# Differential attention: four of nine probability blocks per query group multiplied with V in plain fp32

## The chip, the cores and the metric

One core of a Trainium2 chip runs the whole kernel. The metric is the device time of one execution in microseconds (us). Its engines are PE (TensorE: matmuls, with weight loads shown apart as PEld), DVE (VectorE), ACT (ScalarE), POOL (GpSimd) and SP (SyncE, which issues all DMAs here). Each engine takes its instructions in the order in which the program lists them.

## What is computed

One layer of a diffusion transformer with differential attention: 2048 latent tokens, 256 context tokens, width 1024, 8 heads. Each head has two score maps over 2304 keys; their softmaxes are subtracted with a weight and the result is multiplied with that head's values.

```python
q, k, v, z = split(rms_norm(x) * (1 + sc) + sh) @ w_in        # latent and context; rope on latent q, k
p = softmax(einsum('bqhzd,bkhzd->bhzqk', q * d**-0.5, k))
a = p[:, :, 0] - lam * p[:, :, 1]                             # 2048 x 2304 for each of 8 heads
o = einsum('bhqk,bkhe->bqhe', a, v)
o = o * rsqrt(mean(o*o) + eps) * subln_gain * (1 - lambda_init)
x = x + gt * ((o * silu(z)) @ w_out)                          # then a last rms_norm
```

## The kernel before, in words

All numbers are fp32. A product of two fp32 matrices is made on PE from three products of fp32r tiles, a format to which the producer of a tile rounds it: `hi` is the rounded value, `lo` is what is left (x - hi), and hi*hi + hi*lo + lo*hi is summed in PSUM.

Three stages follow one another. **project** (L178) normalizes the tokens, multiplies them with `w_in`, and writes q, k, v and the gate to scratch in DRAM. Values come from `mm_rows` (L423): 128 tokens x 256 columns (two heads) at a time, two such in a PSUM tile of 512 columns, that is 256 keys of two heads. There are 9 such tiles for each of 4 pairs of heads. `split_steps` (L481) cuts each into `hl` (high by ACT in `cut_high`, low by DVE in `cut_low`), and `store_rows` (L466) writes both halves to `v_d`, one DMA per head.

**attend** (L628) runs 64 query groups: 8 heads, and 8 groups of 256 queries in each. For a group there are 12 steps `qk` (four matmuls of 384 columns into one of two PSUM tiles `s`), each emptied by a `keep` on DVE (L683); exponentials on ACT (L701); a weight and a sum on POOL (L711, L715). The joined matrix, 256 queries x 2304 keys, is then taken in 9 blocks of 256 keys. For each block, `turn` transposes four 128x128 pieces on PE (L722) into a PSUM tile `t`; `high` copies it to an fp32r tile `hi` on ACT (L730); `low` makes t - hi on DVE (L735); and `pv` (L737) multiplies: for each of two key tiles three fp32r matmuls with 256 moving columns, the weights being V's high half (twice) and low half. Everything of a group accumulates in one PSUM tile `po`. `sumsq` (L773) is the one pair of matmuls that comes once in a group. After a head's eight groups, `mean` (L801 to L806) and `root` turn the sums of squares into a factor; these run among the next head's groups. During the last head, the gates of the first 512 tokens of heads 0 to 6 are worked in as well (`mul1` POOL L940, `mul2` DVE L944, `high` ACT L950, `low` DVE L954). **finish** (L957) is the output projection.

V of a head lies in SBUF, in one of two tiles `v`: high and low halves of 18 key tiles. `load_v` (L651) is called for heads 0 and 1 ahead of the loop, and for head h+2 after the last `pv` of head h. The same two tiles later hold output weights.

The order on each engine is set by `Plan.order` (L128): every step has a nominal length in ns, a due time, and buffers that it takes and gives back; a free engine starts the step that is due first among those whose inputs and buffers are there by the plan's own clock. For blocks these are

```python
step("low", "DVE", 602, due + 0.6, low, (g, b), [("high", g, b)], take=["LO"], give=["T"])
step("pv", "PE", 654, due + 2, pv, (g, b), [("low", g, b)] + first, give=["HI", "LO"])
```

with 3 buffers T (PSUM), 4 HI and 4 LO (SBUF).

Of the kernel before, what the change touches and what calls it, by code (L numbers as in the profile page):

```python
# [12 lines left out]
F32 = mybir.dt.float32  # L13
F32R = mybir.dt.float32r
# [6 lines left out]
P = 128  # L21
D = 1024
# [3 lines left out]
KEYS = LAT + CTX  # L26
KT = KEYS // P
# [13 lines left out]
S_BUFS = 2  # L41
T_BUFS = 3
A_BUFS = 6
TP_BUFS = 4
GD = 15
MIX, L3 = (1, 2), 15
XH, WH = 7, 7
# [3 lines left out]
def f32(ap):  # L51
    return ap.bitcast(F32)


def build(tc, x, c, ctx, c_ctx, norm_gain, ada_w, ada_b, final_gain, w_in,
          lam_q, lam_k, subln_gain, w_out, cos_t, sin_t, out):
    nc = tc.nc
    with ExitStack() as top:
        cp = top.enter_context(tc.tile_pool(name="const", bufs=1))
        dr = top.enter_context(tc.tile_pool(name="scratch", bufs=1, space=DRAM))  # L60

        q_d = [dr.tile([P, 2, LAT], F32, name=f"qd{h}") for h in range(H)]
        k_d = [dr.tile([P, 2, KEYS], F32, name=f"kd{h}") for h in range(H)]
        v_d = [dr.tile([P, 2, KT, P], F32, name=f"vd{h}") for h in range(H)]
# [12 lines left out]
        nc.vector.tensor_copy(ones, sums)  # L77
        mhalf = cp.tile([P, 16], F32, name="mhalf")
        nc.vector.memset(mhalf, -0.5)
        sgain = cp.tile([P, 1], F32, name="sgain")  # L80
        neglam = cp.tile([P, 1], F32, name="neglam")

        early = SimpleNamespace(qstack=top.enter_context(ExitStack()), kstack=top.enter_context(ExitStack()))

        def attend_early():
            early.qp = early.qstack.enter_context(tc.tile_pool(name="qp", bufs=1, side="right"))
            early.kp = early.kstack.enter_context(tc.tile_pool(name="kp0", bufs=1, side="right"))
            early.k = load_k(nc, early.kp, k_d, 0)
            early.q = load_q(nc, early.qp, q_d, 0)

        with ExitStack() as ph:
            project(tc, ph, attend_early, ones, x, ctx, c, c_ctx, norm_gain, ada_w, ada_b, w_in, lam_q, lam_k, subln_gain,
                    cos_t, sin_t, ident, mhalf, sgain, neglam, gt_d, q_d, k_d, v_d, gate_d, w_out, wo_d, sums)

        last = Last(tc, gate_d, o_d, f_d, wo_d)
        ph = top.enter_context(ExitStack())
        with ExitStack() as inner:
            attend(tc, ph, inner, early, last, ident, ones, mhalf, sums, neglam, q_d, k_d, v_d, o_d, s_d, f_d)
# [18 lines left out]

# [58 lines left out]


def project(tc, ph, attend_early, ones, x, ctx, c, c_ctx, norm_gain, ada_w, ada_b, w_in, lam_q, lam_k, subln_gain,  # L178
            cos_t, sin_t, ident, mhalf, sgain, neglam, gt_d, q_d, k_d, v_d, gate_d, w_out, wo_d, sums):
# [43 lines left out]

    tiles = {}

    # conditioning
    def cond_silu():
        nc.scalar.activation(rows[0:16], rows[0:16], AF.Silu)

# [79 lines left out]
        step("aturn", "PE", 120, due + 6, ada_turn, (n,), [("arow", n)], take=["AT"], give=["BR"], name=("aturn", n))  # L309
        step("acol", "DVE", 70, due + 6, ada_col, (n,), [("aturn", n)], give=["AT"])  # L310

    # rms norm, modulation and transposition of a block of tokens
    def x_load(b, t):
        src, row, nt = b.src
        xt = tiles["x", b.name, t] = xp.tile([P, D], F32, tag="x", name=f"x{b.name}_{t}", bufs=XB)
# [150 lines left out]
    def store_rows(nm, h, kt):  # L466
        hl = f32(tiles["hl", nm]).rearrange("p f (k u e) -> p f k u e", k=2, u=2)
        for u in range(2):
            nc.sync.dma_start(v_d[h + u][:, :, kt:kt + 2], hl[:, :, :, u])

    def z_silu(nm):
        gz = tiles["z", nm] = zp.tile([P, 512], F32, tag="z", name=f"z{nm}")
# [57 lines left out]
    for half, blks in enumerate(passes):  # L530
        for hpair in range(H // 2):
# [3 lines left out]
            for which, use in turns:  # L535
# [12 lines left out]
                for b in use:  # L548
# [7 lines left out]
                    for cc in range(nt // 2 if which == "v" else 2):  # L556
# [3 lines left out]
                        if which == "v":  # L560
                            for t in range(2):
                                step("mm", "PE", 2620, clock, mm_rows, (nm, w, b, 2 * cc, t), ready,
                                     take=["M"] if t == 0 else [], give=give if t == 1 else [], name=("mm", nm, t))
                                clock += 2.62
                            split_steps(nm, "m", 512, clock, [("mm", nm, 1)], ["M"], store_rows,
                                        (2 * hpair, b.key // P + 2 * cc))
# [58 lines left out]
    return qt  # L625


def attend(tc, ph, inner, early, last, ident, ones, mhalf, sums, neglam, q_d, k_d, v_d, o_d, s_d, f_d):  # L628
# [20 lines left out]
    unit = {}  # L649

    def load_v(h):  # L651
        head[h].v = vp.tile([P, 2, KT, P], F32R, tag="v", name=f"v{h}")
        for z in range(2):
            nc.sync.dma_start(f32(head[h].v[:, z]), v_d[h][:, z])

    def qk(g, u, z, ck):
        h, i = divmod(g, NG)
# [74 lines left out]
    def low(g, b):  # L732
        t = group[g].t[b]
        t[2] = tp.tile([P, 512], F32R, tag="lo", name=f"lo{g}_{b}")
        nc.vector.tensor_tensor(t[2], t[0], f32(t[1]), op=ALU.subtract)  # L735

    def pv(g, b):  # L737
        h = g // NG
        po = po2[:, g % 2]
        pt, hi, lo = group[g].t.pop(b)  # L740
        for e in range(KPER):
            kt = b * KPER + e
            for n, (vi, tt) in enumerate(((0, hi), (0, lo), (1, hi))):
                nc.tensor.matmul(po, head[h].v[:, vi, kt], tt[:, e * GQ:(e + 1) * GQ],  # L744
                                 start=(kt == 0 and n == 0), stop=(kt == KT - 1 and n == 2))
        if b == NB - 1 and g % NG == NG - 1 and h + 2 < H:
            load_v(h + 2)

# [69 lines left out]
        nc.vector.tensor_copy(ft, head[h].m[:n, :P])  # L818
        nc.sync.dma_start(f_d[h], ft)

    plan = Plan(S=S_BUFS, T=T_BUFS, A=A_BUFS, B=2, HI=TP_BUFS, LO=TP_BUFS, O=2)
    done = {}

    def step(kind, engine, cost, due, fn, args, deps=(), take=(), give=()):
# [3 lines left out]
    for g in range(TOTAL):  # L828
# [15 lines left out]
        for b in range(NB):  # L844
            due = (g + 1) * PER + LAG + b * PER / NB
            step("turn", "PE", 436, due, turn, (g, b), [("join", g, u) for u in range(G)],
                 take=["T"], give=["A"] * G if b == NB - 1 else [])
            step("high", "Activation", 478, due + 0.3, high, (g, b), [("turn", g, b)], take=["HI"])
            step("low", "DVE", 602, due + 0.6, low, (g, b), [("high", g, b)], take=["LO"], give=["T"])
            first = [("evac", g - 2)] if b == 0 and g > 1 else []  # L850
            step("pv", "PE", 654, due + 2, pv, (g, b), [("low", g, b)] + first, give=["HI", "LO"])
        due += 2
        step("evac", "Activation", 264, due + 2, evac, (g,), [("pv", g, NB - 1)])
        step("clamp", "Pool", 1029, due + 6, clamp, (g,), [("evac", g)])
# [33 lines left out]
    last.ps = ps_s  # L888
    last.f_turn, last.f_out = f_turn, f_out
    end = TOTAL * PER  # L890
    kshape, vshape = [P, 2, KEYS], [P, 2, KT, P]
# [11 lines left out]


class Last:
    """The gated and scaled heads that go into the output projection."""

    def __init__(self, tc, gate_d, o_d, f_d, wo_d):
        self.tc, self.nc = tc, tc.nc
# [10 lines left out]

    def weights(self, hs, pool, tag, shape):
        t = pool.tile(shape, F32R, tag=tag, name=f"wo{hs[0]}")
        flat = t.rearrange("p a b -> p (a b)" if len(shape) == 3 else "p a b c -> p (a b c)")
# [230 lines left out]
```

## Time and profile before

| | |
|---|---|
| time of three runs, us | 2357.25, 2364.41, 2365.6 (median 2364.41) |
| profiled execution: span | 2359.8 us (its own time is given as the span alone) |
| instructions | 38159 |
| PE busy / DVE busy / POOL busy / ACT busy | 95% / 73% / 60% / 52% of the span |
| granted TensorE clock, mean | 0.980 |
| project, attend, finish, by the trace | to about 829 us, to about 2169 us, to the end |

The page adds up busy time over three stages that have different limits, so the shares above are means over unlike things; the rows further below go by stage. PE's busy time is modelled from starts, so a PE that is shown as busy need not do as much as it can; the pace of its instructions, from start to start, is read from the chain of waits.

### The profile page before, as it was taken

What the parts mean: (1) busy time and instruction counts of PE and PEld (TensorE: products, weight loads), DVE (VectorE), ACT (ScalarE), POOL (GpSimd) and SP (SyncE); (2) the same over time, 40 slices, a digit from 0 to 9 for tenths busy, and PEclk for the clock granted to TensorE, in tenths of its full rate; (3) what the DMA queues carried; (4) which work ended last, traced back from release to release, by engine and by line L of the source; (5) the groups of instructions that cost most, each with busy time, mean ns of one, the idle gap of its engine ahead of it and who ended that gap; (6) DMA issues with size and microseconds to landing.
All of it is one profiled execution on the core that took longest, in us unless ns stands there. A gap on an engine that the chain in (4) does not pass through costs nothing.

```text
span 2359.8 us, 38159 instructions
## 1 busy us (share of the span) xinstructions
PE 2251.5 (95%) x14353; PEld 2070.0 (88%) x14353; DVE 1711.8 (73%) x3726; ACT 1220.0 (52%) x1717; POOL 1422.9 (60%) x691
## 2 busy tenths in 40 slices
PE   7999999999999989989989989899899899889998
PEld 5988888898888879989989989899899898788777
DVE  5746434453233289999999999999999999995664
ACT  5612312232112167767767767677677676564221
POOL 2523233343223268878878878878788788774643
PEclk9999999999999999999999999999999999899999
DMA  9965645454442251321311412213113114224672
GB/s 309 292 217 194 217 134 183 133 175 144 143 134 98 90 158 35 75 68 40 97 43 35 115 34 65 85 35 75 64 36 90 58 35 117 70 65 172 196 242 102
DMA packets 201166, 275.49 MB, mean 117 GB/s; under 512 B 13469, under 2 KB 147221, under 8 KB 195861
## 3 DMA queue, kind: packets, MB, share of 16 engines
q1 hardware_dynamic: 200980, 273.04, 37.3%
q8 instruction: 113, 1.85, 0.3%
q14 instruction: 73, 0.59, 0.1%
HBM read 184.78 MB, written 88.22 MB: 116 GB/s over the span
## 4 chain that ended last, share of the span: by engine, by line
PE 78%; DVE 12%; DMA 4%; POOL 2%; issue 2%; ACT 1%; SPq 0%; POOLq 0%; ACTq 0%; DVEq 0%
PE s L673 20%; PE po L744 16%; PE t L722 9%; PE py L1003 4%; DVE p L683 3%; DVE lo L735 1%; DVE mk L803 1%; DVE o L944 1%; PE m22vl L431 1%; PE m23vl L431 1%; PE m21vl L431 1%; PE m13vl L431 1%; PE m12vl L431 1%; PE m11vl L431 1%; PE m20vl L431 1%
## 5 line engine op out<-in xcount | busy, mean ns | idle before, releaser
L683 DVE TENSOR_SCALAR_CACHE_REDUCE p<-s 128x768 f32<-128x768 f32 x768 | 725.3, 949 | 92.9 <-PE s L673 88.2
L673 PE MATMUL s<-k,q 128*128 128x384 f32 x3072 | 702.0, 355 | 53.4 <-DVE p L683 51.0
L701 ACT ACTIVATE p<-p,st 128x2304 f32<-128x2304 f32 x256 | 569.7, 2225 | 233.1 <-DVE st L690 233.0
L715 POOL TENSOR_TENSOR p<-p,p 128x2304 f32<-128x2304 f32 x128 | 661.7, 5170 | 10.5
L673 PEld LDWEIGHTS s<-k,q 128*128 128x128 f32 x3072 | 513.3, 192 | 74.0 <-DVE p L683 70.1
L744 PE MATMUL po<-hi,v 128*128 128x256 f32 x2304 | 524.6, 291 | 0.3 <-ACT hi L730 0.2
L711 POOL TENSOR_SCALAR p<-p,st 128x2304 f32<-128x2304 f32 x128 | 282.6, 2208 | 250.8 <-DVE st L706 157.9
L744 PEld LDWEIGHTS po<-hi,v 128*128 128x128 f32 x2304 | 401.0, 192 | 4.5 <-ACT ot L752 2.1
L735 DVE TENSOR_TENSOR lo<-t,hi 128x512 fp32r<-128x512 f32 x576 | 392.9, 684 | 10.6 <-ACT hi L730 9.3
L730 ACT CAST hi<-t 128x512 fp32r<-128x512 f32 x576 | 319.7, 582 | 130.8 <-PE t L722 129.8
L722 PE MATMUL t<-ident,p 128*128 128x128 f32 x2304 | 347.6, 275 | 4.1 <-POOL p L715 4.1
L744 PE MATMUL po<-lo,v 128*128 128x256 f32 x1152 | 329.0, 286 | 14.9 <-DVE lo L735 14.9
L722 PEld LDWEIGHTS t<-ident,p 128*128 128x128 f32 x2304 | 277.9, 142 | 13.6 <-POOL p L715 4.9
L744 PEld LDWEIGHTS po<-lo,v 128*128 128x128 f32 x1152 | 221.7, 192 | 17.0 <-DVE lo L735 16.6
L1003 PE MATMUL py<-wo,gh 128*128 128x512 f32 (+1 forms) x528 | 163.7, 392 | 4.0 <-ACT gh L950 4.0
L1003 PEld LDWEIGHTS py<-wo,gh 128*128 128x128 f32 x528 | 98.7, 189 | 27.1 <-ACT gh L950 4.9
L1003 PE MATMUL py<-wo,gl 128*128 128x512 f32 (+1 forms) x264 | 103.6, 392 | 1.3 <-DVE gl L954 1.3
L950 ACT CAST gh<-o 128x512 fp32r<-128x512 f32 x32 | 19.8, 620 | 106.4 <-DVE o L944 103.4
L940 POOL TENSOR_TENSOR o<-o,f 128x512 f32<-128x512 f32 x32 | 42.8, 1338 | 42.4 <-DMA o<-od 33.4
L1016 POOL TENSOR_TENSOR fv<-fv,fx 128x512 f32<-128x512 f32 x30 | 42.6, 1435 | 39.8 <-DVE fv L1011 36.7
L944 DVE TENSOR_TENSOR o<-o,gate 128x512 f32<-128x512 f32 x32 | 47.2, 1477 | 26.3 <-POOL o L940 26.3
L683 DVE DVE_READ_ACCUMULATOR p<-s 128x1 f32 x768 | 62.4, 81 | 0.0
(592 smaller groups left out, 3936.6 us busy)
## 6 DMA issues: line engine op xcount, KB each, us to landing
q<-qd SPq DMA_DIRECT2D x256, 128.0 KB
k<-kd SPq DMA_DIRECT2D x32, 576.0 KB
v<-vd SPq DMA_DIRECT2D x16, 1152.0 KB
aw<-in_ada_w SPq DMA_DIRECT2D x12, 1024.0 KB
xl<-in_x SPq DMA_DIRECT2D x16, 512.0 KB
wod<-hlwo SPq DMA_DIRECT2D x16, 512.0 KB
od<-ot SPq DMA_DIRECT2D x64, 128.0 KB
o<-od SPq DMA_DIRECT2D x32, 256.0 KB
```

Source lines behind the costliest of these rows:

```text
L431: nc.tensor.matmul(tiles["m", nm][:, t * 256:(t + 1) * 256], tok[:, j, ts], ww[:, j], start=(i == 0), stop=(i == 3 * NCH - 1))
L673: nc.tensor.matmul(ps[:, b, :CK // 2], group[g].q[:, z, f, u * P:(u + 1) * P], head[h].k[:, z, k0:k0 + CK // 2], start=(f == 0), stop=(f = ...
L683: nc.vector.tensor_scalar(un.p[z][:, ck * CK:(ck + 1) * CK].rearrange("p (b k) -> p b k", b=2), un.s[z, ck][:, :, :CK // 2], -0.125, None, ...
L701: nc.scalar.activation(un.p[z], un.p[z], AF.Exp, bias=un.st[:, 6 + z:7 + z], scale=-1.0, accum_out=acc)
L711: nc.gpsimd.tensor_scalar(p[1], p[1], unit[g, u].st[:, 9:10], 1.0, op0=ALU.mult, op1=ALU.mult)
L715: nc.gpsimd.tensor_tensor(p[0], p[0], p[1], op=ALU.add)
L722: nc.tensor.transpose(pt[:, (e * G + u) * P:(e * G + u + 1) * P], unit[g, u].p[0][:, kt * P:(kt + 1) * P], ident)
L730: nc.scalar.copy(t[1], t[0])
L735: nc.vector.tensor_tensor(t[2], t[0], f32(t[1]), op=ALU.subtract)
L744: nc.tensor.matmul(po, head[h].v[:, vi, kt], tt[:, e * GQ:(e + 1) * GQ], start=(kt == 0 and n == 0), stop=(kt == KT - 1 and n == 2))
L944: self.nc.vector.tensor_tensor(t.o, t.o, t.gate, op=ALU.mult)
L1003: nc.tensor.matmul(py[r, i], aa[:, ts], w[h][:, f, sl], start=(h == 0 and n == 0), stop=(h == H - 1 and n == 2))
```

## The change

Of the nine blocks b of a group, those in `WHOLE` = (1, 3, 5, 7) are no longer cut. ACT copies the transposed block to an fp32 tile (`whole`), and `pv` issues two plain fp32 matmuls of 256 columns for it, one per key tile, with V as plain fp32 weights, in place of six fp32r ones. The step `low` is left out for them, and their PSUM tile T is given back by ACT's copy. The five other blocks are as before. In project, the value tiles of the four blocks are copied once by ACT and stored as fp32 (`keep_rows`, `store_whole`) in place of the cut into halves. The `v` tile of a head has 20 half tiles and 8 whole ones, in place of 36 half tiles; it is loaded with three DMAs in place of two. HI and LO have 3 buffers each in place of 4, and the new tiles have 3. In the plan, `pv` is given 870 ns for a whole block and 700 in place of 654 for a cut one; a whole block's `pv` depends on `high` alone.

```diff
-TP_BUFS = 4
+TP_BUFS = 3
+WHOLE = (1, 3, 5, 7)
+SPLIT = tuple(b for b in range(KT // 2) if b not in WHOLE)
+VS, VW = 2 * len(SPLIT), 2 * len(WHOLE)
+VN = max((2 * VS + VW) * P, 4 * D)
+N_BUFS = 3
...
+    def keep_rows(nm):
+        tiles["vw", nm] = ep.tile([P, 2, 512], F32, tag="hl", name=f"vw{nm}")
+        nc.scalar.copy(tiles["vw", nm][:, 0], tiles["m", nm])
...
     def load_v(h):
-        head[h].v = vp.tile([P, 2, KT, P], F32R, tag="v", name=f"v{h}")
+        v = vp.tile([P, VN], F32R, tag="v", name=f"v{h}")
+        head[h].v = v[:, :2 * VS * P].rearrange("p (f k e) -> p f k e", f=2, k=VS)
+        head[h].vw = f32(v[:, 2 * VS * P:(2 * VS + VW) * P]).rearrange("p (k e) -> p k e", k=VW)
         for z in range(2):
             nc.sync.dma_start(f32(head[h].v[:, z]), v_d[h][:, z])
+        nc.sync.dma_start(head[h].vw, vw_d[h])
...
+    def whole(g, b):
+        t = group[g].t[b]
+        t[1] = tp.tile([P, 512], F32, tag="whole", name=f"tw{g}_{b}", bufs=N_BUFS)
+        nc.scalar.copy(t[1], t[0])
...
         for e in range(KPER):
-            kt = b * KPER + e
+            es = slice(e * GQ, (e + 1) * GQ)
+            if b in WHOLE:
+                kt = KPER * WHOLE.index(b) + e
+                nc.tensor.matmul(po, head[h].vw[:, kt], hi[:, es], start=False, stop=False)
+                continue
+            kt = KPER * SPLIT.index(b) + e
...
+            if b in WHOLE:
+                step("high", "Activation", 478, due + 0.3, whole, (g, b), [("turn", g, b)], take=["NT"], give=["T"])
+                step("pv", "PE", 870, due + 2, pv, (g, b), [("high", g, b)], give=["NT"])
+                continue
...
-            step("pv", "PE", 654, due + 2, pv, (g, b), [("low", g, b)] + first, give=["HI", "LO"])
+            step("pv", "PE", 700, due + 2, pv, (g, b), [("low", g, b)] + first, give=["HI", "LO"])
```

## Rows read from the trace of the kernel before

**Rows 1.** Busy time by stretch; columns: stretch, length, busy time (count), clock, DMA.
```profile
core 0: us, PE busy (x) PEld busy (x) DVE busy (x) ACT busy (x) POOL busy (x), PEclk, DMA share, GB/s
500.00:700.00 200.00, 200.00 (x1110) 175.47 (x1109) 70.26 (x102) 40.72 (x56) 60.67 (x44) 1.00 0.47 149
...
1913.00:1952.00 39.00, 39.00 (x285) 38.10 (x285) 36.39 (x96) 29.33 (x41) 31.84 (x13) 1.00 0.13 38
1970.00:2117.00 147.00, 125.19 (x835) 121.18 (x834) 140.96 (x297) 91.88 (x125) 108.05 (x45) 0.92 0.27 79
```

**Rows 2.** Chain that ended last, shares of the span by engine (page).
```profile
PE 78%; DVE 12%; DMA 4%; POOL 2%; issue 2%; ACT 1%; SPq 0%; POOLq 0%; ACTq 0%; DVEq 0%
```

**Rows 3.** The same chain inside one group: start, length, what ran.
```profile
1313.22 0.23 PE pss L773 x2
1313.45 1.41 PE s L673 x8
1314.86 0.44 PE t L722 x4
1315.30 0.71 PE po L744 x6
...
1332.45 0.23 PE pss L773 x2
```

**Rows 4.** Waits of all engines, 1200 to 1800 us: total, times, longest.
```profile
DVE p L683 <- PE s L673: 35.7, 88, 1.4
...
PE s L673 <- DVE p L683: 26.9, 4, 6.7
```

**Rows 5.** Groups of instructions, 1200 to 1800 us: count, busy, mean ns, idle before.
```profile
L735 DVE TENSOR_TENSOR lo<-t,hi 128x512 fp32r<-128x512 f32 x265 | 180.9, 684 | 0.8
...
L730 ACT CAST hi<-t 128x512 fp32r<-128x512 f32 x264 | 146.5, 583 | 58.7 <-PE t L722 58.2
```

**Rows 6.** Line L431, one set of 256-column matmuls: duration, first and last start.
```profile
L431 PE MATMUL m12vl<-wh12v,hil x64: 277/283/283, 313.3 to 336.0; 128*128 128x256 f32 x64
```

**Rows 7.** The chain in project: matmuls of 512 columns.
```profile
807.19 21.77 PE m23zl L419 x96
```

**Rows 8.** Starts of L773, once per group: steady pair, a change of head, last head.
```profile
1188.58 0.40 PE L773 MATMUL pss<-sh,ones 128*2 128x256 f32 x2
...
1255.53 0.48 PE L773 MATMUL pss<-sh,ones 128*2 128x256 f32 x2
...
1926.34 0.40 PE L773 MATMUL pss<-sh,ones 128*2 128x256 f32 x2
1945.49 0.40 PE L773 MATMUL pss<-sh,ones 128*2 128x256 f32 x2
...
2116.82 0.41 PE L773 MATMUL pss<-sh,ones 128*2 128x256 f32 x2
```

**Rows 9.** Timeline of DVE and PE at a change of head: start, length.
```profile
1036.24 2.10 DVE L801 SCALAR_TENSOR_TENSOR u<-ssq,r 128x16 f32<-128x16 f32 x1
1038.59 4.89 DVE L803 TENSOR_SCALAR mk<-u 128x16 f32<-128x16 f32 x1
...
1044.91 1.65 PE L673 MATMUL s<-k,q 128*128 128x384 f32 x4 [6.72 <-DVE p L683]
```

**Rows 10.** Timeline of POOL at the same place.
```profile
1036.13 2.19 POOL L711 TENSOR_SCALAR p<-p,st 128x2304 f32<-128x2304 f32 x1 [1.05 <-DVE ssq L791]
1038.40 5.05 POOL L715 TENSOR_TENSOR p<-p,p 128x2304 f32<-128x2304 f32 x1
```

**Rows 11.** Waits of PE, 1940 to 2150 us (last head).
```profile
PE po L744 <- DVE lo L735: 14.9, 6, 3.1
PE s L673 <- DVE p L683: 7.8, 2, 6.9
```

**Rows 12.** Timeline of DVE in the last head.
```profile
2006.30 4.19 DVE L944 TENSOR_TENSOR o<-o,gate 128x512 f32<-128x512 f32 x1
```

**Rows 13.** Waits 800 to 862 us (start of attend).
```profile
PE s L673 <- DMA q<-qd: 1.6, 2, 1.4
```

More of the change, by code (lines that the diff above doesn't have):

```diff
@@ L63, in build @@
         k_d = [dr.tile([P, 2, KEYS], F32, name=f"kd{h}") for h in range(H)]
-        v_d = [dr.tile([P, 2, KT, P], F32, name=f"vd{h}") for h in range(H)]
+        v_d = [dr.tile([P, 2, VS, P], F32, name=f"vd{h}") for h in range(H)]
+        vw_d = [dr.tile([P, VW, P], F32, name=f"vwd{h}") for h in range(H)]
         gate_d = [dr.tile([P, LAT], F32, name=f"gate{h}") for h in range(H)]
@@ L92, in build @@
             project(tc, ph, attend_early, ones, x, ctx, c, c_ctx, norm_gain, ada_w, ada_b, w_in, lam_q, lam_k, subln_gain,
-                    cos_t, sin_t, ident, mhalf, sgain, neglam, gt_d, q_d, k_d, v_d, gate_d, w_out, wo_d, sums)
+                    cos_t, sin_t, ident, mhalf, sgain, neglam, gt_d, q_d, k_d, v_d, vw_d, gate_d, w_out, wo_d, sums)
         last = Last(tc, gate_d, o_d, f_d, wo_d)
@@ L97, in build @@
         with ExitStack() as inner:
-            attend(tc, ph, inner, early, last, ident, ones, mhalf, sums, neglam, q_d, k_d, v_d, o_d, s_d, f_d)
+            attend(tc, ph, inner, early, last, ident, ones, mhalf, sums, neglam, q_d, k_d, v_d, vw_d, o_d, s_d, f_d)
         with ExitStack() as inner:
@@ L178, in project @@
 def project(tc, ph, attend_early, ones, x, ctx, c, c_ctx, norm_gain, ada_w, ada_b, w_in, lam_q, lam_k, subln_gain,
-            cos_t, sin_t, ident, mhalf, sgain, neglam, gt_d, q_d, k_d, v_d, gate_d, w_out, wo_d, sums):
+            cos_t, sin_t, ident, mhalf, sgain, neglam, gt_d, q_d, k_d, v_d, vw_d, gate_d, w_out, wo_d, sums):
     nc = tc.nc
@@ L464, in store_cols, with store_rows, store_whole @@
         nc.sync.dma_start(dst[:, :, o:o + n], f32(tiles["hl", nm][:, :, :n]))
-    def store_rows(nm, h, kt):
+    def store_rows(nm, h, b):
         hl = f32(tiles["hl", nm]).rearrange("p f (k u e) -> p f k u e", k=2, u=2)
+        at = 2 * SPLIT.index(b)
         for u in range(2):
-            nc.sync.dma_start(v_d[h + u][:, :, kt:kt + 2], hl[:, :, :, u])
+            nc.sync.dma_start(v_d[h + u][:, :, at:at + 2], hl[:, :, :, u])
+    def keep_rows(nm):
+        tiles["vw", nm] = ep.tile([P, 2, 512], F32, tag="hl", name=f"vw{nm}")
+        nc.scalar.copy(tiles["vw", nm][:, 0], tiles["m", nm])
+    def store_whole(nm, h, b):
+        t = tiles["vw", nm][:, 0].rearrange("p (k u e) -> p k u e", k=2, u=2)
+        at = 2 * WHOLE.index(b)
+        for u in range(2):
+            nc.sync.dma_start(vw_d[h + u][:, at:at + 2], t[:, :, u])
     def z_silu(nm):
@@ L564, in project @@
                                 clock += 2.62
-                            split_steps(nm, "m", 512, clock, [("mm", nm, 1)], ["M"], store_rows,
-                                        (2 * hpair, b.key // P + 2 * cc))
+                            at = b.key // P // 2 + cc
+                            if at in WHOLE:
+                                step("cut1", "Activation", 533, clock, keep_rows, (nm,), [("mm", nm, 1)],
+                                     take=["S"], give=["M"], name=("cut1", nm))
+                                step("store", "SP", 900, clock + 1, store_whole, (nm, 2 * hpair, at), [("cut1", nm)],
+                                     give=["S"], name=("store", nm))
+                            else:
+                                split_steps(nm, "m", 512, clock, [("mm", nm, 1)], ["M"], store_rows,
+                                            (2 * hpair, at))
                             continue
@@ L625, in load_q, with attend @@
     return qt
-def attend(tc, ph, inner, early, last, ident, ones, mhalf, sums, neglam, q_d, k_d, v_d, o_d, s_d, f_d):
+def attend(tc, ph, inner, early, last, ident, ones, mhalf, sums, neglam, q_d, k_d, v_d, vw_d, o_d, s_d, f_d):
     nc = tc.nc
@@ L741, in pv @@
         for e in range(KPER):
-            kt = b * KPER + e
+            es = slice(e * GQ, (e + 1) * GQ)
[4 more added lines that the diff above has]
+            kt = KPER * SPLIT.index(b) + e
             for n, (vi, tt) in enumerate(((0, hi), (0, lo), (1, hi))):
-                nc.tensor.matmul(po, head[h].v[:, vi, kt], tt[:, e * GQ:(e + 1) * GQ],
-                                 start=(kt == 0 and n == 0), stop=(kt == KT - 1 and n == 2))
+                nc.tensor.matmul(po, head[h].v[:, vi, kt], tt[:, es],
+                                 start=(kt == 0 and n == 0), stop=(kt == VS - 1 and n == 2))
         if b == NB - 1 and g % NG == NG - 1 and h + 2 < H:
@@ L819, in f_out @@
         nc.sync.dma_start(f_d[h], ft)
-    plan = Plan(S=S_BUFS, T=T_BUFS, A=A_BUFS, B=2, HI=TP_BUFS, LO=TP_BUFS, O=2)
+    plan = Plan(S=S_BUFS, T=T_BUFS, A=A_BUFS, B=2, HI=TP_BUFS, LO=TP_BUFS, NT=N_BUFS, O=2)
     done = {}
@@ L847, in attend @@
                  take=["T"], give=["A"] * G if b == NB - 1 else [])
+            first = [("evac", g - 2)] if b == 0 and g > 1 else []
+            if b in WHOLE:
+                step("high", "Activation", 478, due + 0.3, whole, (g, b), [("turn", g, b)], take=["NT"], give=["T"])
+                step("pv", "PE", 870, due + 2, pv, (g, b), [("high", g, b)], give=["NT"])
+                continue
             step("high", "Activation", 478, due + 0.3, high, (g, b), [("turn", g, b)], take=["HI"])
             step("low", "DVE", 602, due + 0.6, low, (g, b), [("high", g, b)], take=["LO"], give=["T"])
-            first = [("evac", g - 2)] if b == 0 and g > 1 else []
-            step("pv", "PE", 654, due + 2, pv, (g, b), [("low", g, b)] + first, give=["HI", "LO"])
+            step("pv", "PE", 700, due + 2, pv, (g, b), [("low", g, b)] + first, give=["HI", "LO"])
         due += 2
@@ L890, in attend @@
     end = TOTAL * PER
-    kshape, vshape = [P, 2, KEYS], [P, 2, KT, P]
+    kshape, vshape = [P, 2, KEYS], [P, VN]
     step("wload", "SP", 5900, end, last.weights, ((0, 1), kp, "k", kshape), [("qk", TOTAL - 1, G - 1, 1, NC - 1)])
@@ L922, in weights @@
         t = pool.tile(shape, F32R, tag=tag, name=f"wo{hs[0]}")
-        flat = t.rearrange("p a b -> p (a b)" if len(shape) == 3 else "p a b c -> p (a b c)")
+        flat = t.rearrange("p a b -> p (a b)") if len(shape) == 3 else t
         for i, h in enumerate(hs):
```

## The prediction

> **What bounds the kernel now.** I read the busy time by stretch first, then the chain that ended last, then the waits, and the pace of PE's instructions last. In project PE is busy all of the time and every other engine less than half of it [rows 1]; the same holds for PE in the steady part of attend, but there DVE is close behind: 36.39 of 39 us, against 39.00 for PE. So two engines are nearly full, and the question is which of them sets the pace. The chain says PE, with 78% of the span against DVE's 12% [rows 2]. Inside one group it is PE alone, one piece starting where the last ended: four transposes 0.44 us, a block's six value matmuls 0.71 us, eight score matmuls 1.41 us, from one L773 to the next in 19.23 us [rows 3]. The waits agree: in 600 us PE waited for DVE in four places only, 26.9 us, none longer than 6.7, while DVE waited for PE 88 times [rows 4]. PE's pace there is also its own and not one that DVE imposes: six matmuls of 256 columns in 0.71 us are 0.119 us each, and in project, where DVE has time to spare, 190 such matmuls start between 313.3 and 336.0 us, 0.120 each [rows 6].
>
> Two places are different. At each of six changes of head DVE's small instructions L801 and L803 last 2.10 and 4.89 us, each until POOL's L711 and L715 end beside them, and PE then stands 6.72 us behind a `keep` [rows 9, 10]. Three groups across a change of head take 1255.53 - 1188.58 = 66.95 us, and three steady ones 3 x 19.15 = 57.45 [rows 8], so one change costs 9.5 us, what PE loses at the lower clock behind the stop included. And in the last head DVE is full, 140.96 of 147 us with PE at 125.19 and the clock at 0.92 [rows 1], since it has L944 and L954 to do too, and L944 can take 4.19 us [rows 12]; PE waits there for `lo` six times, 14.9 us [rows 11]. From 1945.49 seven groups go by until 2116.82: 171.3 us, against 7 x 19.15 = 134.1 [rows 8]. Less one change of head, 27.8 us are DVE's overload.
>
> **The change part by part.** The removed matmuls are six per whole block at 0.119, 0.714 us. There are 4 x 64 = 256 whole blocks, and DVE loses as many `low` steps of 0.684 us [rows 5], 2.74 us in a group.
>
> *The two plain fp32 matmuls* are nowhere in the trace of before. Only the transposes read fp32 that no one rounded, 128 columns each at 0.44 / 4 = 0.109 us [rows 3]; at that rate per column 256 columns take 0.219, and a block 0.437. That is the lower end. For the upper end I take four fp32r matmuls of the same width for one plain one, hi and lo of either operand against each other: 4 x 0.119 = 0.476, a block 0.952. Between them: 512 columns take 21.77 / 96 = 0.2268 us [rows 7], so 256 further columns cost 0.108 and the fixed part of a matmul is 0.011. Four streams of 256 columns with one fixed part are 4 x 0.108 + 0.011 = 0.442, a block 0.884. I take this one, nearer the upper end: what the kernel spends three products on, a plain product must do at least as completely, and the lengths that the plan is given, 870 for two against 654 for six before, have the same ratio of four to one per matmul (they are no measurement, though `turn` has 436 there and takes 0.44). Price per block 0.884 - 0.714 = +0.170 us (ends -0.277 and +0.238).
>
> The Trainium skill, page "FP8 and Floating Point Precision", section "TensorE Precision Notes", states four passes through the array for true FP32. No row here shows a plain fp32 product; by that page the sum would be the one that I take.
>
> *On the path* this counts in full wherever PE sets the pace: 57 groups outside the seven of the last head, 57 x 4 x 0.170 = +38.8 us. DVE falling from 36.39 to about 31 us in such a stretch gives nothing back there, since PE hardly waited for it.
>
> *In the seven groups of the last head* DVE sets the pace, so 28 removed `low` steps can shorten them by up to 28 x 0.684 = 19.2 us; PE's floor there, 134.1 + 28 x 0.170 + 9.5 = 148.4, is 22.9 below the 171.3 and lies lower still. The least is nothing, if it is the single long L944 that stops PE (a block that is still cut waits for `lo` behind it just as long) and not the sum of DVE's work. I take -14, since five of nine blocks still wait for `lo` while DVE's backlog shrinks by 2.74 us in each group.
>
> *The changes of head* I cost at nothing. PE stands behind `keep`, which needs L803 to end, and none of this is edited. But the order on the engines is planned anew, and L801 and L803 are long only because POOL's L711 and L715 start just ahead of them; if they fell elsewhere, a change could cost between 0 and 9.5 us less, and as well some us more if both met an L715 (5.05 us) from its start. Ends: -57 and +18 for six.
>
> *Waits and buffers.* A whole block's `pv` waits for ACT's copy alone; ACT is busy 29.33 of 39 us and its copy stays 0.583 us [rows 1, 5], so a wait that was not visible at the later `lo` is not to be expected at the earlier `hi`. Behind a waiting `pv` the next `qk` would be queued on PE, and DVE's `keep` behind that. T comes back one step earlier for four of nine blocks. Three HI and LO for five cut blocks in nine reach further than four for nine. Nothing, both ways, within what PE waited before.
>
> *Project* loses 16 of its `cut_low` steps on DVE, which works 70 of 200 us beside a PE that is full [rows 1], and stores half the bytes for those tiles. Nothing on the path; the cover is PE itself.
>
> *Loads.* The V loads of heads 0 and 1 are issued ahead of the next q, for which PE waits 1.6 us at the start of attend [rows 13]. Each head's V shrinks from 36 to 28 tiles of 64 KB. At most these 1.6 us are won; I take -1. The third DMA per head adds an issue on SP's queue, against which no engine stands.
>
> **Sum:** +38.8 - 14 - 1 = +24 us. The profiled execution is given by its span, 2359.8 us, 4.6 below the median of the runs shown, which spread over 8.4; I add the sum to the median: 2364.4 + 24 = 2388 us. What is late next is PE as before, now at 19.15 + 4 x 0.170 = 19.83 us a group.
>
> **The rivals.** *Cheap fp32*: the plain matmul streams at the rate of the transposes, 0.219 us. Place: the 256 whole blocks. It saves 0.277 x 4 in each of 57 groups, 63 us, and the last head gains up to 17 more: 2364.4 - 63 - 17 - 1 = 2283. For it speaks that transposes do read full fp32 at that rate; against it that they make no product of two full operands. It decides for faster from the price at which 228 blocks no longer cost more than the 15 us won elsewhere: (0.714 + 15 / 228) / 2 = 0.39 us a matmul. The Trainium skill, page "Perfetto Trace Analysis", section "Engine Utilization", puts the output rate of FP32_LOW_HIGH at half; read as the whole price that gives, as an estimate, 0.22 us for a matmul of 256 columns, and no row shows it for a product.
>
> *Changes of head get cheaper*: the new order moves L801 and L803 away from POOL's two instructions, and most of the 6.7 us stops go: 2388 - 6 x 5 = 2358, no change. For it: the stops are chance meetings; against it: the four in 600 us cost 26.9 us and none over 6.7 [rows 4], so the plan puts them there, and due times are not edited.
>
> *Dear fp32*: weight loads, hidden behind matmuls now, show up beside the passes. With two at the pace of a transpose, 0.109, a matmul takes 0.476 + 0.219 = 0.695 and a block 1.39: 228 x 0.676 = +154 us, and the last head becomes PE's, 28 x 0.676 - 27.8 = -9: about 2509. For it: two halves of the weights must come in; against it: a load has 0.2 us of matmul to hide behind.
>
> **How the numbers follow.** Forecast 0.69, its own range 2368 to 2412: the price between 0.43 and 0.476, the last head between nothing and -19. Cheap fp32 0.09, cheaper changes of head 0.14, dear fp32 0.08. The range 2354 to 2414 leaves out cheap and dear fp32 and the tails. Half a per cent, about what a measurement of this kernel can tell from no change, is 12 us. Faster: cheap fp32 and a third of the cheaper changes, 0.13. Within: the rest of those and the low tail of the forecast, 0.17. Slower: 0.70.
>
> **What would show it.** The pace of the two new matmuls from start to start: 0.43 to 0.48 us. L773 to L773 in a steady group: 19.8 us, PE without gaps, DVE near 15.1 us of it. The seven groups of the last head: near 157 us with fewer waits for `lo`. The stops at changes of head: 6.7 us again. It is wrong if the price is under 0.39, if steady groups show PE waiting for ACT's copy, or if the last head gives back more than the 38.8 us that the others lose.

## The result and the profile after

The changed kernel takes 2388.6 us (median; 2379.4 to 2389.8) against 2362.8 for the kernel before on the same chip: a ratio of 1.0107, 95% interval 1.0085 to 1.0129, slower by about 26 us. The forecast was 2388. The number came out as forecast, in part by luck: the forecast cost of the first 52 groups was 12.4 us too high, the gain before them 6.4 us too small, and the last head, forecast 14 us shorter, grew by 8.3; these errors made up for one another. One run each of two later experiments, of 7087 and 7618 us, is a slow one and is left out of the medians below. The profiled executions have spans of 2359.8 and 2388.0 us, 28.2 apart, and the rest of this section follows these 28.2.

Busy time by stretch, with the columns of [rows 1]: the same stretch of project, a steady one of attend, and the last head.

```profile
500.00:700.00 200.00, 200.00 (x1109) 175.46 (x1108) 68.29 (x98) 40.79 (x56) 61.33 (x45) 1.00 0.46 145
1929.00:1968.00 39.00, 39.00 (x265) 37.49 (x264) 31.35 (x85) 29.54 (x41) 31.52 (x13) 1.00 0.12 35
1961.00:2141.00 180.00, 151.43 (x932) 142.23 (x930) 154.64 (x319) 109.00 (x149) 127.70 (x53) 0.91 0.29 82
```

In the steady stretch DVE has fallen from 36.39 to 31.35 of 39 us, and PE is as full as before. The chain's shares by engine (page), beside [rows 2], say the same: PE 78% has become 86%, DVE 12% has become 7%.

```profile
PE 86%; DVE 7%; POOL 3%; issue 2%; DMA 1%; ACT 0%; SPq 0%; POOLq 0%; DVEq 0%; ACTq 0%
```

Inside one group the chain is PE alone, as in [rows 3]; L700 is the old L673, L749 the old L722, L810 the old L773. L777 is the pair of plain products, L781 a cut block.

```profile
1312.63 0.72 PE po L781 x6
1313.34 0.87 PE po L777 x4
1314.21 0.70 PE s L700 x4
1314.91 0.44 PE t L749 x4
1315.35 0.24 PE pss L810 x2
...
1334.99 0.24 PE pss L810 x2
```

A whole block takes 0.87 us in four matmuls: each plain product shows as two MATMULs with a weight load each, about 0.216 us apart, so a product takes 0.43 us; 0.442 was forecast. From one L810 to the next it is 19.64 us here. The line itself (duration, first and last start) counts 1024 such MATMULs, four for each of 256 blocks:

```profile
L777 PE MATMUL po<-tw,v x1024: 377/379/634, 854.5 to 2189.9; 128*128 128x256 f32 x171
```

The starts of L810, which answer to [rows 8]: first group, the three groups across a change of head, the beginning of the last head's seven groups and their end.

```profile
884.15 0.48 PE L810 MATMUL pss<-sh,ones 128*2 128x256 f32 x2
...
1187.76 0.48 PE L810 MATMUL pss<-sh,ones 128*2 128x256 f32 x2
...
1256.34 0.48 PE L810 MATMUL pss<-sh,ones 128*2 128x256 f32 x2
...
1961.10 0.48 PE L810 MATMUL pss<-sh,ones 128*2 128x256 f32 x2
...
2140.74 0.49 PE L810 MATMUL pss<-sh,ones 128*2 128x256 f32 x2
```

With the same starts of before (891.54, 1945.49, 2116.82) the 28.2 us divide as follows; the forecast's +38.8 is 52 groups at 0.68 and 5 at the end. The "seven groups of the last head" are those from the 53rd to the 60th sum of squares, three of the seventh head and four of the last. The first start of before is

```profile
891.54 0.40 PE L773 MATMUL pss<-sh,ones 128*2 128x256 f32 x2
```

| stretch | before | after | change | forecast |
|---|---|---|---|---|
| start to the first sum of squares | 891.5 | 884.2 | -7.4 | -1 |
| 52 groups | 1053.9 | 1077.0 | +23.0 | +35.4 |
| seven groups of the last head | 171.3 | 179.6 | +8.3 | -14 |
| from there to the end | 243.0 | 247.3 | +4.3 | +3.4 |

Of the last row's 4.3 us, 1.5 lie in the last four groups and 2.8 behind the last sum of squares, in finish, whose work the change leaves as it was; what made them longer is not known.

The stops at changes of head are there as before: 1256.34 - 1187.76 = 68.6 us for three groups, 9.8 over three steady ones of 19.6. PE now stands behind `low` (L762), four times in 600 us as in [rows 4]; in the last head behind `keep` (L710) and `low`, 28.5 us in all against 22.7 [rows 11]. First the waits from 1200 to 1800 us, then PE's from 1940 to 2160.

```profile
DVE p L710 <- PE s L700: 105.6, 148, 1.9
...
PE po L781 <- DVE lo L762: 26.0, 4, 6.5
```
```profile
PE s L700 <- DVE p L710: 19.1, 5, 4.9
PE po L781 <- DVE lo L762: 9.4, 3, 6.1
```

### The profile page after: what moved, and what is told of

It is laid out like the page before. It is cut to its first block, busy times and chain, and to the rows that moved or that the text cites. A ratio compares the mean times of both kernels' runs of the same rounds, so it can differ in the third digit from the quotient of the medians.

```text
span 2388.0 us, 36602 instructions
## 1 busy us (share of the span) xinstructions
PE 2280.0 (95%) x13841; PEld 2074.0 (87%) x13841; DVE 1560.4 (65%) x3454; ACT 1236.0 (52%) x1717; POOL 1419.7 (59%) x691
## 4 chain that ended last, share of the span: by engine, by line
PE 86%; DVE 7%; POOL 3%; issue 2%; DMA 1%; ACT 0%; SPq 0%; POOLq 0%; DVEq 0%; ACTq 0%
PE s L700 21%; PE t L749 10%; PE po L781 9%; PE po L777 9%; PE py L1044 4%; DVE mk L840 1%; DVE o L985 1%; DMA o<-od 1%; DVE p L710 1%; PE m23vl L437 1%; PE m22vl L437 1%; PE m21vl L437 1%; PE m13vl L437 1%; PE m12vl L437 1%; PE m10vl L437 1%
## 5 line engine op out<-in xcount | busy, mean ns | idle before, releaser
L710 DVE TENSOR_SCALAR_CACHE_REDUCE p<-s 128x768 f32<-128x768 f32 x768 | 732.2, 954 | 245.0 <-PE s L700 238.8
L700 PE MATMUL s<-k,q 128*128 128x384 f32 x3072 | 725.0, 361 | 22.6 <-DVE p L710 21.9
L742 POOL TENSOR_TENSOR p<-p,p 128x2304 f32<-128x2304 f32 x128 | 659.9, 5156 | 10.6
L700 PEld LDWEIGHTS s<-k,q 128*128 128x128 f32 x3072 | 522.3, 192 | 38.1 <-DVE p L710 30.4
L738 POOL TENSOR_SCALAR p<-p,st 128x2304 f32<-128x2304 f32 x128 | 282.3, 2206 | 287.4 <-DVE st L733 181.7
L749 PE MATMUL t<-ident,p 128*128 128x128 f32 x2304 | 348.7, 274 | 1.7 <-POOL p L742 1.7
L749 PEld LDWEIGHTS t<-ident,p 128*128 128x128 f32 x2304 | 285.0, 142 | 27.4 <-POOL p L742 2.2
L781 PE MATMUL po<-hi,v 128*128 128x256 f32 x1280 | 288.0, 287 | 0.0
L777 PE MATMUL po<-tw,v 128*128 128x256 f32 x1024 | 271.2, 388 | 0.0
L757 ACT CAST hi<-t 128x512 fp32r<-128x512 f32 x320 | 183.9, 575 | 137.0 <-PE t L749 137.0
L781 PE MATMUL po<-lo,v 128*128 128x256 f32 x640 | 184.5, 288 | 48.4 <-DVE lo L762 48.4
L762 DVE TENSOR_TENSOR lo<-t,hi 128x512 fp32r<-128x512 f32 x320 | 219.2, 685 | 16.4 <-ACT hi L757 16.4
L781 PEld LDWEIGHTS po<-hi,v 128*128 128x128 f32 x1280 | 223.9, 193 | 2.1 <-ACT hi L757 0.4
L777 PEld LDWEIGHTS po<-tw,v 128*128 128x128 f32 x1024 | 187.4, 195 | 15.3
L767 ACT COPY tw<-t 128x512 f32<-128x512 f32 x256 | 149.7, 585 | 71.3 <-PE t L749 70.2
L781 PEld LDWEIGHTS po<-lo,v 128*128 128x128 f32 x640 | 123.5, 193 | 50.9 <-DVE lo L762 50.9
```

The source lines that it names most:

```text
L700: nc.tensor.matmul(ps[:, b, :CK // 2], group[g].q[:, z, f, u * P:(u + 1) * P], head[h].k[:, z, k0:k0 + CK // 2], start=(f == 0), stop=(f = ...
L710: nc.vector.tensor_scalar(un.p[z][:, ck * CK:(ck + 1) * CK].rearrange("p (b k) -> p b k", b=2), un.s[z, ck][:, :, :CK // 2], -0.125, None, ...
L738: nc.gpsimd.tensor_scalar(p[1], p[1], unit[g, u].st[:, 9:10], 1.0, op0=ALU.mult, op1=ALU.mult)
L742: nc.gpsimd.tensor_tensor(p[0], p[0], p[1], op=ALU.add)
L749: nc.tensor.transpose(pt[:, (e * G + u) * P:(e * G + u + 1) * P], unit[g, u].p[0][:, kt * P:(kt + 1) * P], ident)
L757: nc.scalar.copy(t[1], t[0])
```

## The experiments

Two theories were open. One: TensorE's price for the plain products makes the loss, and what VectorE no longer does is worth little. The other: the loss comes from the fewer buffers and the new order, or the relief of VectorE is worth more than it seems. The ratios below are to the kernel before on the same chip.

**No block whole.** All nine blocks are cut again, every other edit stays.

```diff
-WHOLE = (1, 3, 5, 7)
+WHOLE = ()
...
```

> The changed kernel with WHOLE empty: all nine blocks are cut again, in project and in attend, while its other edits stay (3 HI and 3 LO buffers, 700 ns for pv in the plan, the tile v in its new form). Theory (the plain products' price on TensorE makes the loss): near the kernel before, 2363 within 6 us, 19.15 to 19.25 us from one L773 to the next in a steady group, project done at 829 us. Rival (the buffers and the newly planned order make it): stays at 2380 to 2390.

2361.6 us, ratio 0.9999 (0.9984 to 1.0015). Steady groups take 19.18 us:

```profile
1275.53 0.40 PE L808 MATMUL pss<-sh,ones 128*2 128x256 f32 x2
1294.71 0.40 PE L808 MATMUL pss<-sh,ones 128*2 128x256 f32 x2
```

The fewer buffers and the 700 ns cost nothing (the third load of V is gone here too); the loss hangs on the whole blocks.

**Seven blocks whole.**

```diff
-WHOLE = (1, 3, 5, 7)
+WHOLE = (1, 2, 3, 4, 5, 6, 7)
...
-N_BUFS = 3
+N_BUFS = 4
```

> WHOLE is 1 to 7, with 4 of the fp32 tiles in place of 3: 448 plain blocks in place of 256. Theory: each further whole block costs TensorE 0.865 - 0.714 = 0.151 us, so a steady group takes 19.6 + 3 x 0.151 = 20.05 to 20.1 us and the time is 2388 + 57 x 0.45 = 2414 within 8. Rival (what VectorE no longer does pays back): 2388 or less.

2402.1 us, ratio 1.0163 (1.0143 to 1.0183); steady groups 20.03 us:

```profile
1270.43 0.48 PE L810 MATMUL pss<-sh,ones 128*2 128x256 f32 x2
1290.46 0.48 PE L810 MATMUL pss<-sh,ones 128*2 128x256 f32 x2
```

Three further blocks cost 20.03 - 19.59 = 0.44 us in a group, 0.147 each, which is the price of the chain (0.865 - 0.714). The time is 12 us below what was expected, and not for one reason. Against the changed kernel's trace, the seven groups of the last head took 169.2 us, ten less although their products cost more, and the six changes of head before them 10 us less together, 7.3 to 8.9 each; the stretch before the first sum of squares took 9.6 us more. The price is confirmed, and the last head is not a matter of it.

**VectorE's work put back.** VectorE makes the difference for whole blocks too; nobody reads it.

```diff
...
+                step("low", "DVE", 602, due + 0.6, spare, (g, b), [("high", g, b)], take=["LO"], give=["T", "LO", "NL"])
...
```

> The changed kernel, in which VectorE makes the difference t - tile for the four whole blocks too, and nothing reads it: the work that the change took from VectorE in attend is back, the plain products stay. Theory: TensorE sets the pace, so little is lost: 0.13 to 0.2 us in a steady group as TensorE stood for VectorE before, 19.65 to 19.8 us, and 2388 to 2402 in all, with project still done at 824 us. Rival (the relief of VectorE is worth as much as its 2.7 us a group suggest): 2420 or more.

2391.1 us, ratio 1.0108 (1.0077 to 1.0138), no different from the changed kernel's 1.0107. Steady groups stay at 19.60 us; DVE is back at 35.48 of 39 us:

```profile
1274.80 0.40 PE L818 MATMUL pss<-sh,ones 128*2 128x256 f32 x2
1294.40 0.40 PE L818 MATMUL pss<-sh,ones 128*2 128x256 f32 x2
```
```profile
1913.00:1952.00 39.00, 39.00 (x265) 37.29 (x264) 35.48 (x93) 29.52 (x41) 31.44 (x13) 1.00 0.12 35
```

The four `low` steps of a group, 2.7 us of VectorE's time, are worth nothing where TensorE sets the pace. The 0.13 to 0.2 us that the theory expected to come back did not (below).

**Plain products replaced by one fp32r product.** The whole blocks and their values are rounded to fp32r and multiplied once; the two products with low halves are left out.

```diff
...
-        t[1] = tp.tile([P, 512], F32, tag="whole", name=f"tw{g}_{b}", bufs=N_BUFS)
+        t[1] = tp.tile([P, 512], F32R, tag="whole", name=f"tw{g}_{b}", bufs=N_BUFS)
...
```

> The whole blocks' tiles and values are rounded to fp32r and multiplied once in that format, so the two low products are left out: the structure of the change at a price of 0.24 us a block in place of 0.865. Theory: a steady group falls to 12 x 0.703 + 9 x 0.437 + 5 x 0.713 + 4 x 0.24 + 0.24 = 17.1 us, up to 17.4 with waits, and the time to 2388 - 57 x 2.4 = 2250 within 12, as neither GpSimd (15.8 us a group) nor VectorE (15.3) is in the way. Rival (another engine or the order holds the group at over 18.5 us): 2320 or more.

2332.0 us, ratio 0.9875 (0.9859 to 0.9891): the rival, not the theory, which was 82 us too low. Groups take 18.77 us, not 17.1. GpSimd's timeline repeats every 18.77 us, each weight L738 waiting for VectorE's ratio L733 and each join L742 following it:

```profile
1407.04 2.20 POOL L738 TENSOR_SCALAR p<-p,st 128x2304 f32<-128x2304 f32 x1 [1.60 <-DVE st L733]
1409.32 5.16 POOL L742 TENSOR_TENSOR p<-p,p 128x2304 f32<-128x2304 f32 x1
...
1425.81 2.19 POOL L738 TENSOR_SCALAR p<-p,st 128x2304 f32<-128x2304 f32 x1 [1.57 <-DVE st L733]
```

I had added up each engine's busy time (GpSimd 15.8 us) and left out the waits in the loop from exponentials to ratio to weight to join. The chain from 1400 to 1440 us agrees: weight and join make 37% of it, TensorE's matmuls 9%. If this loop is as long in the other kernels, which no run tested, TensorE bounds the group of before (19.18) by only 0.4 us.

**The last head.** The gate steps that VectorE ran go to GpSimd.

```diff
-        step("gmul2", "DVE", 602, due + 5, last.mul2, (0, h), [("gmul1", 0, h)])
+        step("gmul2", "Pool", 1250, due + 5, last.mul2, (0, h), [("gmul1", 0, h)])
...
-        step("glow", "DVE", 602, due + 7, last.low, (0, h), [("ghigh", 0, h)], give=["O"])
+        step("glow", "Pool", 1250, due + 7, last.low, (0, h), [("ghigh", 0, h)], give=["O"])
...
```

> The changed kernel with the two gate steps of the last head that VectorE ran (the product with the gate and the difference from the rounded copy, seven times each) moved to GpSimd. Theory: what slows the last head is a VectorE instruction with both operands in SBUF that lasts until GpSimd's instruction beside it ends (up to 5.5 us), not the sum of VectorE's work; in GpSimd's own queue it cannot. The seven groups up to the fourth of the last head then take 7 x 19.62 + 9.7 = 147 us, up to 154, in place of 179.6, and the time is 2389 - 29 = 2360 within 8. Rival (GpSimd, with 14 instructions of 1.3 us more, becomes the bound there): 2380 or more.

2372.4 us, ratio 1.0045 (1.0030 to 1.0060): 16 us better than the changed kernel, halfway between theory and rival. The seven groups take 168.5 us in place of 179.6, not 147 to 154. That VectorE's gate product can last until GpSimd's join beside it has ended is shown by the changed kernel's own timelines, first VectorE, then GpSimd: it ends 0.55 us after the join; alone it takes 0.69 (4.19 in [rows 12]):

```profile
2014.02 5.04 DVE L985 TENSOR_TENSOR o<-o,gate 128x512 f32<-128x512 f32 x1
```
```profile
2013.40 5.11 POOL L742 TENSOR_TENSOR p<-p,p 128x2304 f32<-128x2304 f32 x1
```

Some 21 us over seven steady groups and a change of head stay. The busy time of the same seven groups, in the changed kernel and here, shows a part of them:

```profile
1961.10:2140.70 179.60, 151.03 (x928) 141.89 (x927) 154.24 (x319) 108.60 (x148) 127.70 (x53) 0.91 0.29 82
```
```profile
1962.10:2130.50 168.40, 155.17 (x993) 145.03 (x990) 132.86 (x327) 113.58 (x157) 143.54 (x68) 0.97 0.31 85
```

TensorE does 65 more matmuls here: score matmuls, transposes and blocks of the groups behind have moved in, an estimated 9.4 us at the paces above, and the four groups that follow take 44.7 us in place of 52.8. One gate product is left on VectorE there; it lasts 6.77 us, and TensorE stands 5.8 us behind it. The remaining 6 us or so are open.

**The changes of head.** The small steps after the reciprocal go to GpSimd, in the changed kernel alone, in both kernels together with the gate steps, and in the kernel before alone.

```diff
...
-        nc.vector.tensor_scalar(hd.mk, hd.u, 2.0 ** 72, None, op0=ALU.is_lt)
-        nc.vector.tensor_scalar(hd.u, hd.u, 2.0 ** 72, 2.0 ** 49, op0=ALU.min, op1=ALU.mult)
...
+        nc.gpsimd.tensor_scalar(hd.mk, hd.u, 2.0 ** 72, 1.0, op0=ALU.is_lt, op1=ALU.mult)
+        nc.gpsimd.tensor_scalar(hd.u, hd.u, 2.0 ** 72, 2.0 ** 49, op0=ALU.min, op1=ALU.mult)
...
```

> The changed kernel with the small steps on a head's sums of squares (mean, after the reciprocal) moved from VectorE to GpSimd, where the power that follows already runs. Theory: the stops at the changes of head are VectorE's two small instructions lasting until GpSimd's end; without them a change costs 0 to 2 us in place of 9.7, seven times, so the time is 2389 - 60 = 2329 within 8. Rival (GpSimd's eight small steps delay the next weight and join, and TensorE waits there): 2360 or more.

2335.6 us, ratio 0.9892 (0.9871 to 0.9913), within the expected 8: a change of head costs 2.7 to 4.5 us in place of 8.6 to 10.2. The six changes in the first 52 groups give 37.5 us, less than expected; the seven groups of the last head, with the seventh change in them, give another 19 (160.6 us in place of 179.6), twice what was expected there.

> The kernel before with both moves to GpSimd, the gate steps and the mean steps. Theory: seven changes of head at 9.5 us, less 0 to 2 each, and 27.8 us of the last head go: 2363 - 60 - 26 = 2277 within 10, and steady groups stay at 19.15 to 19.25 us, as TensorE sets their pace. Rival (as above, GpSimd becomes the bound): 2320 or more.

2310.6 us, ratio 0.9787 (0.9770 to 0.9804): 34 us above the theory, short of the rival. The changes of head went nearly as expected (2.0 to 2.2 us each), the last head did not: its seven groups take 164.1 us, 27.8 over seven steady groups and a change, as before. But here too matmuls of later groups have moved in (1032 in the seven groups in place of 984, an estimated 7 us), so the gate steps may well have given about that much.

> The changed kernel with both moves to GpSimd. With VectorE's stops gone from both kernels what is left between them is the price of the plain products. Theory: 0.4 to 0.45 us in each of 60 or so groups, so 22 to 29 us over the kernel before with both moves, less what project may end earlier: 2297 within 10. Rival (the relief of VectorE is worth something once the stops are gone): equal to the kernel before with both moves, or faster.

2328.8 us, ratio 0.9866 (0.9845 to 0.9888): 18.2 over the kernel before with the same moves, where 22 to 29 less an earlier end of project were expected; the expected 2297 was missed by 32, as the kernel that it was added to came out 34 too high. The first sum of squares comes 6.9 us earlier than there, so what follows it takes 25 us more, as expected: with most of VectorE's stops gone the plain products still cost.

> The kernel before with only the mean steps moved to GpSimd. Theory: seven changes of head fall from 9.5 to about 2.5 us, as they did where both moves were made, and the gate steps on VectorE cost what they cost on GpSimd: 2362 - 49 = 2313 within 8, level with the kernel that has both moves (2310.6). Rival (the gate steps on GpSimd were worth the 16 us that they gave in the changed kernel): 2325 or more.

2316.7 us, ratio 0.9811 (0.9789 to 0.9833), within the expected 8 and 6 above the kernel with both moves. The two intervals overlap; the gate steps on GpSimd are worth about that much in the kernel before at most, not 16.

**Order alone.** The changed kernel with other nominal lengths in the plan; not one instruction is added or removed.

```diff
-                step("pv", "PE", 870, due + 2, pv, (g, b), [("high", g, b)], give=["NT"])
+                step("pv", "PE", 813, due + 2, pv, (g, b), [("high", g, b)], give=["NT"])
...
-            step("pv", "PE", 700, due + 2, pv, (g, b), [("low", g, b)] + first, give=["HI", "LO"])
+            step("pv", "PE", 654, due + 2, pv, (g, b), [("low", g, b)] + first, give=["HI", "LO"])
```

> The changed kernel with other nominal lengths for pv in the plan alone: 654 and 813 ns in place of 700 and 870. The same instructions, in another order in attend. Theory: order decides what VectorE's long instructions in the last head stop, so the steady groups stay at 19.6 us, and the stretch from the 53rd L773 to the end (426.9 us in the changed kernel) differs by 3 us or more, either way; the time is 2378 to 2398. Rival (that stretch is set by the work in it): 425 to 429 us there, and 2386 to 2391 in all.

2324.7 us, ratio 0.9847 (0.9811 to 0.9884): 64 us below the changed kernel, which neither side expected. The steady groups are the same 19.59 us. What went are above all the changes of head, 53 us over the first 52 groups: the comparison step (L840, old L803) takes 0.17 us in all eight, and three groups across a change take 59.46 us, 0.7 over three steady ones. The seven groups of the last head, with the seventh change in them, take 172.0 us in place of 179.6. The line, and then the starts:

```profile
L840 DVE TENSOR_SCALAR mk<-u x8: 174/174/176, 1031.2 to 2145.8; 128x16 f32<-128x16 f32 x8
```
```profile
1177.54 0.48 PE L810 MATMUL pss<-sh,ones 128*2 128x256 f32 x2
...
1237.00 0.48 PE L810 MATMUL pss<-sh,ones 128*2 128x256 f32 x2
```

In this order VectorE's small steps stand ahead of the ratio that releases GpSimd's weight and join, so GpSimd is idle beside them; before and after they stand right behind it [rows 9, 10]. VectorE's comparison L840 and ratio L733 at one change of head, first in this order, then in the changed kernel:

```profile
1031.15 0.17 DVE L840 TENSOR_SCALAR mk<-u 128x16 f32<-128x16 f32 x1
...
1031.93 0.27 DVE L733 TENSOR_SCALAR st<-st,neglam,l 128x1 f32<-128x1 f32 x1
```
```profile
1031.95 0.27 DVE L733 TENSOR_SCALAR st<-st,neglam,l 128x1 f32<-128x1 f32 x1
...
1034.85 4.89 DVE L840 TENSOR_SCALAR mk<-u 128x16 f32<-128x16 f32 x1
```

**That order on purpose, in the kernel before.**

```diff
-            step("scols", "DVE", 75, due + 15, ssq_cols, (h,), [("sturn", h)], give=["T"])
-            step("mean", "DVE", 700, due + 15, mean, (h,), [("scols", h)])
+            step("scols", "DVE", 75, due + 14, ssq_cols, (h,), [("sturn", h)], give=["T"])
+            step("mean", "DVE", 700, due + 14, mean, (h,), [("scols", h)])
```

> The kernel before with the due times of the plan's scols and mean steps one unit earlier and nothing else, which puts a head's small VectorE steps ahead of the ratio that releases GpSimd's weight and join. Theory: the small steps L801 and L803 then run beside an idle GpSimd, 0.17 us each in place of 2.1 and 4.9, as in the changed kernel under other plan lengths; a change of head costs 1 to 3 us in place of 9.5, and the time is 2361 - 50 = 2311 within 8. Rival (the place of the ratio is not what makes them long): 2361 within 6.

2312.5 us, ratio 0.9797 (0.9773 to 0.9820), as expected; L803 has a median of 0.26 us and a change of head costs 58.55 - 57.45 = 1.1:

```profile
1178.43 0.40 PE L773 MATMUL pss<-sh,ones 128*2 128x256 f32 x2
...
1236.98 0.40 PE L773 MATMUL pss<-sh,ones 128*2 128x256 f32 x2
```

> As the other, with the gate steps of the last head on GpSimd too. Theory: 5 to 15 us less than with the due times alone, as GpSimd in the last head takes over what VectorE waited for, 2300 within 8: the fastest of all kernels here. Rival (GpSimd's queue holds up the last head as much): no less than with the due times alone.

2306.7 us, ratio 0.9770 (0.9750 to 0.9790): 5.8 less, at the low end of what was expected; the fastest here, 2.3% below the kernel before and, by the ratios, 3.3% below the changed one.

## Why the prediction was right, and where it was not

The main mechanism was right: TensorE's price for the plain products, on the path in every steady group. The size of the sum was luck in part, as the terms show one by one.

*What bounds the kernel*: right. TensorE sets the pace of steady groups before and after, and 0, 4 and 7 whole blocks gave 19.18, 19.6 and 20.03 us a group; VectorE's work put back changed nothing.

*The price of a plain product*: right in kind, 0.43 us measured, 0.442 forecast, +0.151 a block in place of +0.170. The two MATMULs that show for a product take 0.216 us each, twice the 0.108 us that 256 columns add to an fp32r matmul. The Trainium skill, page "FP8 and Floating Point Precision", section "TensorE Precision Notes", states four passes for true FP32. The trace agrees in time: 0.43 us are four times 0.108. The rival of half that price is out.

*On the path, in full in 57 groups*: mis-sized, 23.0 us measured over 52 groups in place of 35.4. The smaller price is 4 us of this, the rest that it did not count in full: four blocks at 0.151 make 0.60 us, and a group grew by 0.44. The chain of the kernel before has the missing part: once in a group two `qk` follow one another in 1.59 us and not in the 1.41 of [rows 3], since the weight loads of the second wait 0.24 us for a `keep`:

```profile
1318.31 1.59 PE s L673 x8
```

In the changed kernel's group all pairs take 1.40 or 1.41. So 0.18 us of a wait was already in the group of before and went, which the prediction counted as PE's own time. It did not come back with VectorE's work, so it did not go with the relief; with no block whole it is there again:

```profile
1290.00 1.59 PE s L698 x8
```

So it goes with the whole blocks, be it by their order or by the time that the longer products leave for the `keep`; the runs do not tell these apart.

*The seven groups of the last head, -14*: wrong, in sign too; +8.3 was measured, of which 7 x 0.44 = 3.1 is the price. The step took a shrinking backlog of VectorE for the cause. Putting that work back left the seven groups at 173.3 us and removing more of it (seven whole blocks) at 169.2, so it is not the sum of VectorE's work; the bound that the prediction named at "nothing", single long instructions, was the better end. VectorE instructions of over 1.3 us make 40.5 us in the changed kernel's seven groups, with TensorE idle for 28.6; 35.5 and 25.0 before; 30.8 and 22.4 with VectorE's work put back. Which of them meets a join changes with the order, and that no view of the kernel before could show. In two other pairs of kernels with and without the change the seven groups differ otherwise: by +4.3 us where order removed the stops at the changes of head (172.0 and 167.7), by -2.6 with both moves to GpSimd (161.4 and 164.0). So what goes beyond the price is not a fixed effect of the change; which stop costs how much is not settled.

*Project, nothing; loads, -1*: -4.6 and -2.8. Project's gain sits in one place, where TensorE stood for VectorE's gate row L290 for 1.98 us and now for 0.96, and the granted clock, 0.78 on average from 210 to 220 us before, around the longer stop, is now 1.00 there, its higher level of 2.4 GHz. The stretch from 190 to 240 us, first before, then after:

```profile
190.00:240.00 50.00, 47.26 (x258) 40.53 (x258) 29.89 (x48) 11.19 (x18) 13.94 (x10) 0.93 0.60 195
```
```profile
190.00:240.00 50.00, 49.04 (x297) 43.24 (x296) 25.47 (x47) 11.50 (x18) 15.01 (x10) 1.00 0.55 183
```

The stretch from the first matmul of `m11kl` to that of `m11vl`, which holds the stop, takes 28.8 us before and 24.1 after, 25.0 with no whole block and 28.1 with seven, so the gain does not follow the number of cuts. The ends of project (824 us with four whole blocks, 831 with none, 833 with seven) say less: four kernels whose project is that of before ended it between 826 and 831. At the start of attend the 1.6 us wait for q is gone; the other 1.2 us were not traced.

*Waits and buffers, nothing*: right; with no block whole the three HI and LO buffers gave a ratio of 0.9999, and no steady group of the changed kernel shows TensorE waiting for ScalarE's copy.

*Changes of head, nothing*: right for this pair, 9.5 and 9.8 us, and right by an accident of order. The ends named, -57 and +18, were fair: nominal lengths that differ by 46 and 57 ns brought -64 in all, 53 of them in the six changes of head. Where the stops are gone from both kernels, by the moves to GpSimd, the change costs 18 us, and where order removed them (2324.7 and 2312.5), 12; the earlier end of project is in both.

## What to carry to other kernels

Read an engine's pace from start to start and count an added cost in full only after looking for the waits inside that pace; here more than a quarter of the price fell into one. Work taken from an engine that is nearly full is worth nothing while another sets the pace: with VectorE busy for 91% and for 80%, the groups of the changed kernel took the same time. And before a few tenths of a per cent are credited to an edit, change only the order of the same instructions: that alone moved this kernel by 2.6%.

## What the runs showed of the hardware

Some VectorE instructions with all operands in SBUF last until the GpSimd instruction beside them ends: L801 and L803 (128x16) take 0.17 us with GpSimd idle, 2.10 beside a weight of 2.19 and 4.89 beside a join of 5.05 [rows 9, 10]. The same holds for a gate product of 128x512, 0.69 us alone and 5.04 beside a join. Not all do so: L690, 128x3 in SBUF, took 0.13 to 0.16 us in all its 256 runs in the kernel before, over 200 of them beside GpSimd's work. What reads PSUM, `keep` and `low`, does not stretch either: 0.93 to 0.96 and 0.67 to 0.69 us throughout. A plain fp32 matmul of 256 columns is two MATMULs of 0.216 us in the trace, where a transpose of fp32 is one, of 0.109 us for 128 columns.
